# The sum over the partitions of a modulation chunk, placed one chunk later

## The chip, the cores and the metric

The kernel runs on one core of one Trainium2 chip. The metric is device time in microseconds (us), from the start of the program to its end. The kernel before takes 983.03 us (median of 3 runs, 981.76 to 984.24). The engines are TensorE (PE, with PEld for its weight loads), VectorE (DVE), ScalarE (ACT), GpSimd (POOL) and SyncE (SP), which issues most of the DMAs.

## What is computed

One layer of an encoder trunk with 512 tokens of width 1024, all in f32. A conditioning vector `c` gives six modulation vectors; each is 1024 long, and the last four of them are what this change is about:

```python
mod = silu(c) @ ada_w + ada_b                     # (1, 6 * 1024)
sh1, sc1, gt1, sh2, sc2, gt2 = split(mod, 6)
h = rmsnorm(x, g1) * (1 + sc1) + sh1
x = x + gt1 * mixer(h)                            # gated delta rule + mLSTM, both directions
h = rmsnorm(x, g2) * (1 + sc2) + sh2
x = x + gt2 * moe(h)                              # 32 experts, two for each token
out = rmsnorm(x, g3)
```

The mixer projects `h` with a wide matrix, runs the two recurrent branches over chunks of the sequence, and joins them. `gt1` is needed at the mixer's end, `sh2`, `sc2` and `gt2` after it.

## The kernel before

The kernel first makes `sh1` and `sc1`, normalises `x`, and begins the projection. One projection tile is 128 output columns for all 512 tokens: 24 matmuls (L347 to L349), eight contraction blocks with three products each of high and low halves of the operands. The halves of a weight tile, `w_hi` and `w_lo`, are split off by DVE, ACT or POOL (L145, L143, L150).

What the change touches lies in the middle of the run, about 190 to 580 us. There five strands of work are woven by a string written out by hand, `ORDER_B` (used at L1188): `g` is a projection tile for a gate, `p` prepares the delta rule's inverse, `s` is a step of its scan (L1033 to L1094), `m` is a step of the mLSTM (L821 to L955), and `d` is one chunk of the later modulation vectors. The strand `d` occurs 16 times: once as the first letter, then after twelve `g` and more, and then at ever shorter distances. `ORDER_C` follows with the rest of `m`, the first output branch `f` and operands `b`, and after it `mod_rows` (L803).

A chunk `q` (of 16, 256 columns of one modulation vector) goes like this. SP loads two halves of the weight's chunk, `aw`, of 512 KB each (L781, two buffers). Eight blocks of 128 rows are multiplied by a column of `silu(c)` and added up, with the rows on the partitions. In eleven chunks DVE does this in one accumulator `ac` (L788 for the first block, L790 for the other seven; one buffer). In chunks 2, 6, 14 and 15 ACT multiplies in place (L786) and DVE adds (L792, L795, L796); in chunk 4 ACT multiplies and POOL adds. In these five the sum stays in `aw` itself. Then TensorE sums over the partitions with a column of ones (L800; the profile shows four matmuls and four weight loads for a chunk, since f32 goes in two passes), and DVE copies the two columns of the result from PSUM into `mcols` (L801). `mod_rows` turns `mcols` (L806), adds the bias and writes the vectors to DRAM, from where `modb` and others are loaded (L1222).

The order on each engine in this part isn't the program's. It is worked out when the program is built, by a planner that has an estimated cost for each instruction: an instruction that stands earlier in the program goes first when both could start, and one that isn't ready by the planner's reckoning is passed over for a later one that is. On the chip each engine then takes its instructions strictly in that order, and waits where an operand isn't there yet. A buffer of a tile pool is given to the next tile once the last reader of the old one is done, so the first write into `ac` (L788) of a chunk comes after the sum (L800) of the chunk that had the buffer before.

Of the kernel before, what the change touches and what calls it, by code (L numbers as in the profile page):

```python
# [7 lines left out]
F32 = mybir.dt.float32  # L8
# [3 lines left out]
OP = mybir.AluOpType  # L12
# [91 lines left out]
def hybrid_kernel(tc, ins, out, consts_in):  # L104
    nc = tc.nc
    ctx = ExitStack()
    with ctx:
        _body(tc, nc, ctx, ins, out, consts_in)


def _body(tc, nc, ctx, ins, out, consts_in):
# [4 lines left out]
    def eng(key, default, choices):  # L116

        return CHOICE.get(key, default)
# [8 lines left out]
    def ps(tag, shape=None):  # L127
        uid[0] += 1
        n, b = psum["tags"][tag]
        return psum["pool"].tile([128, n], F32, name=f"ps_{tag}{uid[0]}", tag=tag, bufs=b)  # L130
# [6 lines left out]
    def nb(key, default, *choices):  # L137
        return eng("#" + key, default, (default,) + choices)
# [233 lines left out]
    for d in range(2):  # L372
# [16 lines left out]
                    op=OP.mult)  # L389
# [371 lines left out]
    pmd = stM.enter_context(tc.tile_pool(name="modw", bufs=1, side="right"))  # L761
# [9 lines left out]
    def mod_chunk(q):  # L771
        i, c0 = q // 4, (q % 4) * 256
        blk = MODS[i]
        o = blk * D + c0
        way = eng(f"mod{q}", "v", "vab")
        wt = []
        if way == "v":
            acc = pmd.tile([128, 256], F32, name=f"ac{q}", tag="ac", bufs=nb("ac", 1, 2))
        for h in range(2):
            w = pmd.tile([128, 4, 256], F32, name=f"aw{q}_{h}", tag="aw", bufs=nb("aw", 2, 3))  # L780
            DMA.dma_start(w, ada_w[h * 512:h * 512 + 512, o:o + 256].rearrange("(k p) n -> p k n", p=128))  # L781
            wt.append(w)
            for k in range(4):
                kk = h * 4 + k
                if way != "v":
                    A.activation(w[:, k], w[:, k], AF.Copy, scale=cT[:, kk:kk + 1])  # L786
                elif kk == 0:
                    V.tensor_scalar(acc, w[:, k], cT[:, kk:kk + 1], None, op0=OP.mult)  # L788
                else:
                    V.scalar_tensor_tensor(acc, w[:, k], cT[:, kk:kk + 1], acc, op0=OP.mult, op1=OP.add)  # L790
            if way != "v":
                (V if way == "a" else G).tensor_tensor(w[:, 0:2], w[:, 0:2], w[:, 2:4], op=OP.add)  # L792
        if way != "v":
            E = V if way == "a" else G
            E.tensor_tensor(wt[0][:, 0:2], wt[0][:, 0:2], wt[1][:, 0:2], op=OP.add)  # L795
            E.tensor_tensor(wt[0][:, 0], wt[0][:, 0], wt[0][:, 1], op=OP.add)  # L796
            acc = wt[0][:, 0]
        p = ps("m")
        for j in range(2):
            PE.matmul(p[:, j:j + 1], acc[:, j * 128:j * 128 + 128], ones[:, 0:1], start=True, stop=True)  # L800
        V.tensor_copy(mcols[:, q * 2:q * 2 + 2], p[:, 0:2])  # L801
# [7 lines left out]
        DMA.dma_start(mdr.rearrange("i (k p) -> (i k) p", p=128), mrow2[:, 0])  # L809

    def mod_chunks():
        for q in range(16):
            mod_chunk(q)
            yield

    stB = ctx.enter_context(ExitStack())
    pb = stB.enter_context(tc.tile_pool(name="mlstm", bufs=1, side="right"))
# [357 lines left out]
    def second_branch():  # L1175
# [7 lines left out]
        for j2 in range(4):  # L1183
            branch_out(ins["w_branch_b"][0], 4, j2, merge)
            yield

    todo.update({"p": prep(), "s": scan(), "m": mlstm(), "d": mod_chunks()})
    for c in ORDER_B:  # L1188
        take(todo[c], 1)
# [844 lines left out]
    last = NT - 1  # L2034
# [58 lines left out]
```

## Time and profile before

| what | value |
|---|---|
| median of 3 runs | 983.03 us (981.76 to 984.24) |
| profiled execution | 980.42 us, its span 978.6 us |
| PE busy | 814.2 us (83%) |
| DVE busy | 660.8 us (68%) |
| ACT, POOL busy | 328.1 us, 316.6 us |
| granted TensorE clock, mean | 0.924 of full speed |
| all L790 (DVE, 77 times) | 44.0 us, mean 572 ns |

The span runs from the first to the last instruction of the profiled execution. A busy time is the union of an engine's instructions, and a share is of the span. The shares hide that the stages differ: in the middle part DVE is busier than PE, and from 530 us on PE is.

### The profile page before, as it was taken

To read this page: it belongs to the slowest core of one execution; us is meant where nothing else is said; L and a number is where in the kernel's file an instruction comes from. 1 tells how busy PE (TensorE), PEld (TensorE's weight loads), DVE (VectorE), ACT (ScalarE), POOL (GpSimd) and SP (SyncE) were. 2 spreads that over 40 slices of the span, in tenths; PEclk is the share of its full clock that TensorE was granted. 3 is DMA by queue.
4 is the path that set the end of the run, shared out by engine and by line. 5 is a ranking of instruction groups with operands and counts; after the bars stand their busy time and mean duration, and the time that the engine had idled before them with its cause. 6 is when DMAs were issued, how large, how long until landed. Compare 5 with 4: busy or idle time off the path is not lost.

```text
span 978.6 us, 16538 instructions
## 1 busy us (share of the span) xinstructions
PE 814.2 (83%) x6204; PEld 595.0 (61%) x6204; DVE 660.8 (68%) x1246; ACT 328.1 (34%) x611; POOL 316.6 (32%) x236
## 2 busy tenths in 40 slices
PE   4799979979486999988797998987699999999840
PEld 3367656768375777866675776776456555555420
DVE  1459999799959999888888888459965322221215
ACT  5435475223101342321334231125522323333203
POOL 0321365214224442563236252323112212111125
PEclk9799999989786999998898999998899999999985
DMA  9932564975265365654474254946689999999965
GB/s 307 270 88 71 108 119 97 204 206 180 58 143 158 87 216 146 181 171 142 150 220 149 94 157 132 369 166 215 237 288 358 351 371 403 414 417 413 415 259 211
DMA packets 171709, 213.80 MB, mean 218 GB/s; under 512 B 47368, under 2 KB 129828, under 8 KB 171628
## 3 DMA queue, kind: packets, MB, share of 16 engines
q1 hardware_dynamic: 167340, 204.33, 64.6%
q0 software_dynamic: 4288, 8.41, 2.4%
q8 instruction: 49, 0.80, 0.3%
q14 instruction: 32, 0.26, 0.1%
HBM read 190.79 MB, written 25.54 MB: 221 GB/s over the span
## 4 chain that ended last, share of the span: by engine, by line
PE 41%; DVE 31%; DMA 16%; issue 5%; POOL 3%; ACT 2%; SPq 1%; POOLq 0%; DVEq 0%; ACTq 0%
DMA wr<-in_w_gate_dram 5%; PE ps_m L1705 5%; DMA wr<-in_w_up_dram 4%; PE ps_acc L348 3%; PE ps_acc L347 3%; PE ps_acc L349 3%; DMA wr<-in_w_down_dram 3%; DVE gu L740 2%; PE ps_m L1708 2%; PE ps_d L1736 2%; DVE ac L790 2%; DVE tt L742 2%; DVE ca L573 1%; PE ps_m L902 1%; DMA hb<-h1d 1%
## 5 line engine op out<-in xcount | busy, mean ns | idle before, releaser
L349 PE MATMUL ps_acc<-hn_hi,w_lo 128*128 128x512 f32 x352 | 142.6, 405 | 16.2 <-DVE w_lo L150 15.4
L347 PE MATMUL ps_acc<-hn_hi,w_hi 128*128 128x512 f32 x352 | 145.5, 413 | 1.8 <-DVE w_hi L145 1.3
L348 PE MATMUL ps_acc<-hn_lo,w_hi 128*128 128x512 f32 x352 | 145.0, 412 | 0.0
L1705 PE MATMUL ps_m<-wr,xin 128*64 128x256 f32 x1024 | 124.4, 390 | 6.1 <-ACT xin L1695 4.2
L150 POOL TENSOR_TENSOR w_lo<-w_raw,w_hi 128x1024 fp32r<-128x1024 f32 x34 | 88.1, 2590 | 103.2 <-ACT w_hi L143 80.9
L1714 DVE SCALAR_TENSOR_TENSOR act<-act,ps_m 64x256 f32<-64x256 f32 (+1 forms) x32 | 14.8, 463 | 133.0 <-ACT act L1713 133.0
L1705 PEld LDWEIGHTS ps_m<-wr,xin 128*64 128x64 f32 x1024 | 75.0, 139 | 43.3 <-issue 6.8
L349 PEld LDWEIGHTS ps_acc<-hn_hi,w_lo 128*128 128x128 f32 x352 | 68.7, 195 | 32.1 <-DVE w_lo L150 16.6
L347 PEld LDWEIGHTS ps_acc<-hn_hi,w_hi 128*128 128x128 f32 x352 | 68.8, 196 | 17.5 <-issue 3.2
L348 PEld LDWEIGHTS ps_acc<-hn_lo,w_hi 128*128 128x128 f32 x352 | 68.8, 195 | 15.6 <-issue 1.5
L1752 POOL DMA_INDIRECT ybuf<-y,idxp x28 | 27.3, 974 | 132.7 <-DVE y L1747 123.8
L1736 PE MATMUL ps_d<-wr,at 128*64 128x512 f32 x256 | 61.3, 598 | 5.2 <-DMA wr<-in_w_down_dram 4.0
L1695 ACT ACTIVATE xin<-xall (+1 forms) x128 | 54.2, 424 | 13.8 <-issue 9.5
L1713 ACT ACTIVATE act<-ps_m 64x256 f32<-64x256 f32 (+1 forms) x32 | 13.4, 418 | 134.7 <-PE ps_m L1705 71.1
L143 ACT ACTIVATE w_hi<-w_raw 128x1024 fp32r<-128x1024 f32 x30 | 31.7, 1058 | 57.3 <-PE ps_acc L348 43.5
L790 DVE SCALAR_TENSOR_TENSOR ac<-aw,cT,ac 128x256 f32<-128x256 f32 x77 | 44.0, 572 | 0.6
L1752 POOL DMA_INDIRECT ybuf<-y,idx x16 | 15.9, 992 | 74.6 <-DVE y L1747 61.1
L1747 DVE TENSOR_TENSOR y<-ps_d,gt 128x512 f32<-128x512 f32 (+1 forms) x32 | 25.3, 792 | 21.4 <-PE ps_d L1736 16.7
L1736 PEld LDWEIGHTS ps_d<-wr,at 128*64 128x64 f32 x256 | 17.4, 136 | 30.0 <-issue 20.1
L1725 PEld LDWEIGHTS ps_m<-ident,act 64*128 64x128 f32 x128 | 16.5, 186 | 22.4 <-DVE act L1715 12.6
L1497 PE MATMUL ps_acc<-woh,yT 128*128 128x512 f32 x64 | 27.5, 430 | 0.0
L740 DVE TENSOR_TENSOR gu<-nn,tt 128x62 f32<-128x62 f32 (+15 forms) x31 | 27.0, 870 | 0.7
(550 smaller groups left out, 1788.0 us busy)
## 6 DMA issues: line engine op xcount, KB each, us to landing
wr<-in_w_gate_dram SPq DMA_DIRECT2D x64, 512.0 KB
wr<-in_w_up_dram SPq DMA_DIRECT2D x64, 512.0 KB
wr<-in_w_down_dram SPq DMA_DIRECT2D x32, 1024.0 KB
w_raw<-in_w_in_dram SPq DMA_DIRECT2D x48, 512.0 KB
aw<-in_ada_w_dram SPq DMA_DIRECT2D x32, 512.0 KB
adaw<-in_ada_w_dram SPq DMA_DIRECT2D x8, 1024.0 KB
gts<-gt SPq DMA_DIRECT2D x20, 256.0 KB
gts<-gts SPq DMA_DIRECT2D x20, 256.0 KB
```

The source lines that it names most:

```text
L143: A.activation(dst, src, AF.Copy, **({} if scale is None else {"scale": scale}))
L150: ENGINE[eng(key, default, choices)].tensor_tensor(dst, a, b, op=op)
L347: PE.matmul(p, hi[:, k], hn_hi[:, k], start=(k == 0), stop=False)
L348: PE.matmul(p, hi[:, k], hn_lo[:, k], start=False, stop=False)
L349: PE.matmul(p, lo[:, k], hn_hi[:, k], start=False, stop=(k == KD - 1))
L740: V.tensor_tensor(o, nn_[:, :, m:, c].unsqueeze(3).to_broadcast([128, 2, n, m]), tt[:, :, c, 0:m].unsqueeze(2).to_broadcast([128, 2, n, m] ...
L790: V.scalar_tensor_tensor(acc, w[:, k], cT[:, kk:kk + 1], acc, op0=OP.mult, op1=OP.add)
L1497: PE.matmul(p, yT[0][:, k, ts], hi[:, k % 2], start=(k == 0), stop=False)
L1695: A.activation(xg[:, :, o], xall[:, :, bass.ds(vs[t], SEG)], AF.Copy)
L1705: PE.matmul(p[64 * b:64 * b + 64, 0:256], xg[:, kk, 0:64], r[:, b], **f)
L1736: PE.matmul(p[64 * c:64 * c + 64, 0:512], at[:, j, 0:64], w[:, j * D + c * 512:j * D + c * 512 + 512], start=(j == 0), stop=(j == 1))
L1752: return G.indirect_dma_start(out=ybuf.rearrange("r (a n) -> (r a) n", a=parts), out_offset=bass.IndirectOffsetOnAxis(ap=ix, axis=0), in_= ...
```

## The change

`mod_chunk(q)` ends with its accumulation and returns the accumulator; the two matmuls and the copy from PSUM become a function of their own, `mod_sum`. The strand `d` calls `mod_sum` for chunk `q-1` right before it issues chunk `q`, and for chunk 15 when the strand is asked once more, after everything in `ORDER_C`. The accumulator `ac` keeps one buffer, and chunks 2, 4, 6, 14 and 15 now write their last addition into it too.

```diff
         wt = []
-        if way == "v":
-            acc = pmd.tile([128, 256], F32, name=f"ac{q}", tag="ac", bufs=nb("ac", 1, 2))
+        acc = pmd.tile([128, 256], F32, name=f"ac{q}", tag="ac", bufs=1)
...
             E.tensor_tensor(wt[0][:, 0:2], wt[0][:, 0:2], wt[1][:, 0:2], op=OP.add)
-            E.tensor_tensor(wt[0][:, 0], wt[0][:, 0], wt[0][:, 1], op=OP.add)
-            acc = wt[0][:, 0]
+            E.tensor_tensor(acc, wt[0][:, 0], wt[0][:, 1], op=OP.add)
+        return acc
+
+    def mod_sum(q, acc):
+
         p = ps("m")
         for j in range(2):
             PE.matmul(p[:, j:j + 1], acc[:, j * 128:j * 128 + 128], ones[:, 0:1], start=True, stop=True)
...
     def mod_chunks():
+        last = None
         for q in range(16):
-            mod_chunk(q)
-            yield
+            if q:
+                mod_sum(q - 1, last)
+            last = mod_chunk(q)
+            yield
+        mod_sum(15, last)
```

## Rows read from the trace of the kernel before

**Rows 1.** The busy time of each engine by stage. The columns are the stretch, its length, then for each engine its busy time and count, then the granted clock, the DMA share and GB/s.

```profile
202.00:268.00 66.00, 52.09 (x220) 42.08 (x220) 64.26 (x75) 16.86 (x26) 20.58 (x9) 0.89 0.49 142
...
330.00:370.00 40.00, 35.78 (x440) 29.60 (x440) 34.84 (x64) 15.17 (x29) 19.22 (x19) 1.00 0.62 185
370.00:400.00 30.00, 29.50 (x188) 24.38 (x186) 29.08 (x54) 10.38 (x17) 8.51 (x5) 1.00 0.55 156
...
420.00:450.00 30.00, 21.95 (x125) 17.47 (x125) 27.39 (x42) 5.92 (x9) 15.42 (x10) 0.89 0.46 138
450.00:482.00 32.00, 27.16 (x239) 21.93 (x238) 26.91 (x53) 7.18 (x13) 8.87 (x6) 0.84 0.52 157
...
500.00:530.00 30.00, 23.41 (x143) 19.84 (x144) 26.32 (x43) 12.99 (x28) 14.06 (x12) 0.89 0.56 173
530.00:560.00 30.00, 27.95 (x190) 22.88 (x190) 25.76 (x57) 10.53 (x16) 13.07 (x9) 1.00 0.37 117
560.00:580.00 20.00, 19.94 (x90) 15.80 (x89) 15.95 (x26) 6.45 (x8) 9.40 (x6) 1.00 0.60 165
```

**Rows 2.** The chain that ended last, between 444 and 452 us: start, length, what.

```profile
444.62 1.17 DVE ac L790
...
448.54 0.41 DVE ac L790
449.08 0.99 PE ps_m L800 x4
450.07 0.64 PE ps_acc L347
```

**Rows 3.** The waits of PE between 180 and 530 us: who waited for whom, us in total, times, the longest.

```profile
PE ps_m L800 <- DVE ac L790: 13.4, 4, 4.8
...
PE ps_m L800 <- issue: 5.1, 2, 3.9
```

**Rows 4.** The same of DVE between 196 and 580 us.

```profile
DVE mcols L801 <- PE ps_m L800: 4.5, 6, 1.3
...
DVE z L1077 <- PE ps_c L1069: 2.4, 2, 1.4
```

**Rows 5.** TensorE in order of time around the sum of chunk 9: start, length, operation, and in brackets the idle time before it and what ended it.

```profile
428.20 0.39 PE L348 MATMUL ps_acc<-hn_lo,w_hi 128*128 128x512 f32 x1
432.28 0.58 PE L800 MATMUL ps_m<-ones,ac 128*128 128x1 f32 x4 [3.70 <-DVE ac L790]
432.72 0.49 PE L349 MATMUL ps_acc<-hn_hi,w_lo 128*128 128x512 f32 x1
...
434.20 0.63 PE L347 MATMUL ps_acc<-hn_hi,w_hi 128*128 128x512 f32 x1
```

**Rows 6.** DVE in order of time around the same sum.

```profile
431.66 0.47 DVE L790 SCALAR_TENSOR_TENSOR ac<-aw,cT,ac 128x256 f32<-128x256 f32 x1
...
432.90 0.16 DVE L801 COPY mcols<-ps_m 128x2 f32<-128x2 f32 x1 [0.16 <-PE ps_m L800]
432.98 0.35 DVE L788 TENSOR_SCALAR ac<-aw,cT 128x256 f32<-128x256 f32 x1
```

**Rows 7.** The sum of chunk 0 on TensorE, and its copy on DVE.

```profile
201.32 0.99 PE L800 MATMUL ps_m<-ones,ac 128*128 128x1 f32 x4 [3.91 <-issue]
...
202.34 0.16 DVE L801 COPY mcols<-ps_m 128x2 f32<-128x2 f32 x1 [0.77 <-PE ps_m L800]
```

**Rows 8.** Chunk 1: the last block of its accumulation on DVE, and its sum on TensorE.

```profile
217.35 0.48 DVE L790 SCALAR_TENSOR_TENSOR ac<-aw,cT,ac 128x256 f32<-128x256 f32 x1
...
290.49 0.61 PE L800 MATMUL ps_m<-ones,ac 128*128 128x1 f32 x4
```

**Rows 9.** Chunk 4's last addition on POOL and its sum on TensorE; the first and the last block of chunk 5 on DVE and its sum.

```profile
337.73 1.70 POOL L796 TENSOR_TENSOR aw<-aw 128x256 f32<-128x256 f32 x1
...
369.16 0.50 PE L800 MATMUL ps_m<-ones,aw 128*128 128x1 f32 x4
...
343.59 0.35 DVE L788 TENSOR_SCALAR ac<-aw,cT 128x256 f32<-128x256 f32 x1
...
361.25 1.50 DVE L790 SCALAR_TENSOR_TENSOR ac<-aw,cT,ac 128x256 f32<-128x256 f32 x1
...
373.67 0.50 PE L800 MATMUL ps_m<-ones,ac 128*128 128x1 f32 x4
```

**Rows 10.** Line L790 alone by stage: the stretch, its length, DVE's busy time in it and the count, clock, DMA.

```profile
290.00:330.00 40.00, 6.19 (x7) 0.79 0.46 126
330.00:370.00 40.00, 4.29 (x7) 1.00 0.62 185
370.00:400.00 30.00, 3.35 (x7) 1.00 0.55 156
```

**Rows 11.** The end of the strand: chunk 15's additions on DVE, its sum on TensorE, and the turning of `mcols`.

```profile
502.85 1.29 DVE L792 TENSOR_TENSOR aw<-aw 128x512 f32<-128x512 f32 x2
...
507.29 1.22 DVE L795 TENSOR_TENSOR aw<-aw,aw 128x512 f32<-128x512 f32 x1
...
508.96 0.42 DVE L796 TENSOR_TENSOR aw<-aw 128x256 f32<-128x256 f32 x1
...
525.62 0.85 PE L800 MATMUL ps_m<-ones,aw 128*128 128x1 f32 x4
...
577.10 0.27 PE L806 MATMUL ps_m<-ident,mcols 128*32 128x128 f32 x1
```

## The prediction

> **What bounds the kernel now.** Read first the busy time by stage. From 202 to 268 us DVE works 64.26 us of 66 and PE 52.09; from 420 to 482 us DVE works 54.30 of 62 (27.39 and 26.91) and PE 49.11; from 530 us PE takes over, with 27.95 of 30 and then 19.94 of 20, while DVE has 25.76 and 15.95 [rows 1]. So in the part where the sixteen chunks run DVE is the bound, and after it PE. Second, the chain of waits at 444 to 452 us: a DVE multiply-add of a chunk (L790), then its sum on PE (L800), then a projection matmul [rows 2]. The chain goes over from DVE to PE at a chunk's sum. Third, the waits. PE stood 13.4 us in four waits for L790 and 5.1 us in two more, put down to "issue", all ahead of L800 [rows 3]. DVE stood far less because of it: 4.5 us at the copy L801 and 2.4 us at the scan's L1077 [rows 4]. As DVE is the bound there, these 6.9 us are what the sums cost at most, and not the 18.5 us of PE.
>
> Two things about the order matter. Chunk 9's sum stands in the middle of a projection tile, between L348 and L349, and PE waits 3.70 us for it [rows 5]: the planner put it where it took the accumulation to be done, and DVE was later. Chunk 1's sum on the other hand ran at 290.49 us although its accumulation had ended at 217.83, and chunk 4's at 369.16 though ready at 339.43 [rows 8, 9]: there PE had work of earlier rank, and the sum waited for its turn in the program. So a sum is late by its rank when DVE is ahead, and early by the planner's reckoning when DVE is behind. The change lowers the rank. It acts on the first kind directly, and on the second only if it makes the accumulation start no later.
>
> **The change, part by part.** The same 64 matmuls, 16 copies and 5 last additions run; nothing is added but the place of five results, and the cost of that is nil (the same operands and shape). I work against the profiled execution, 980.42 us with a span of 978.6 and so 1.82 us outside it. The median shown, 983.03, lies 2.61 above it; differences are added to the median.
>
> *Chunk 0.* Its sum loses its rank to twelve gate tiles, but at 201.32 us PE had been idle for 3.91 us, as the first gate tile's weights weren't split yet. An idle engine is given what is ready, so I expect the sum in the same place. The copy L801, now of a later rank, goes behind the splitting of the weights; DVE's wait of 0.77 us [rows 7] goes: 0.8 us off a stage in which DVE has 1.74 us to spare. If I am wrong and the sum goes behind the gate tiles, chunk 1's accumulation can't start before about 290 us, and eight operations at about 0.48 us, 3.8 us, leave that stage for a later one in which DVE is the bound too: nothing won in sum. From 0 to -3.8 us; I take -0.8.
>
> *The accumulator.* It has one buffer, and L788 of a chunk writes it first. Before, it followed at once on the sum and copy of the chunk ahead (432.28, 432.90, 432.98) [rows 5, 6]. Now sum `q-1` has the rank of chunk `q`, and so has L788 of chunk `q` behind it. Sum, accumulation, sum: this ring is what it was, one place later. For chunks 8 to 13, where DVE is behind, PE has passed their ranks already, and lowering them by one chunk doesn't move the sum: it is still put where the planner takes it for ready. I expect the waits of 3.70 us and the like to remain, at other chunks. From all 4.5 + 2.4 us won to nothing; I take nothing.
>
> *Chunks 4 and 5.* Chunk 4's sum stays in `aw` now, so chunk 5 could begin on `ac` at 343.59 us and end at 362.75. After the change chunk 4's result takes `ac`, its sum has chunk 5's rank, 369 to 374 us, and chunk 5 can't begin until then [rows 9]. Its 0.35 + 4.29 us [rows 9, 10] leave a stage in which DVE is busy 34.84 of 40 for one of 29.08 of 30 or 27.39 of 30 [rows 1]. What one stage wins the next pays: nothing, unless the same operations take longer there. They took 6.19 us for seven at 290 to 330 us and 3.35 at 370 to 400 [rows 10], so that one chunk can cost 2.8 us more or, from 4.29, 0.9 us less: -0.9 to +2.8, and I take nothing, as the stage it goes to has the cheap row.
>
> [...]
>
> *Behind them.* Chunk 5's start moves from 343.59 to 369.66 us at the earliest, the end of chunk 4's sum [rows 9], 26 us. If the chunks behind it keep that delay, sum 15, at 525.62, comes at 552 us. `mod_rows` turns the result at 577.10 [rows 11], so 25 us of cover remain. If they were gone, PE would wait for L806 in its order, microsecond for microsecond. Chunk 15's additions, 1.29 + 1.22 + 0.42 = 2.93 us [rows 11], would leave the stretch 500 to 530 for one bound by PE. DVE idles 3.68 us of that stretch anyway, so I take half, -1.5 us, with ends at 0 and -2.9.
>
> *The queues.* SP gets the loads of `aw` in an order that the planner makes anew; the loads of chunks 3, 7 and 15 no longer wait for a sum, but for the last addition, which waits for the sum before. One wait stands for the other: 0. Behind L788 on DVE are conv, scan and mLSTM work, which wait with it as they did with L801.
>
> The sum: -0.8 + 0 + 0 - 1.5 + 0 = -2.3, and 983.03 - 2.3 = 980.7 us.
>
> **The rivals.**
>
> *The waits go.* If the lowered ranks do put the sums behind their accumulations, DVE gets back its 4.5 and 2.4 us, and with the 1.5 of the strand's end the time is 983.0 - 8.4 = 974.6. For it: after the wait for chunk 9, whose stretch had a granted clock of 0.89, projection matmuls took 0.63 us where they took 0.39 before it [rows 1, 5], so a shorter wait frees more of PE than itself. Against it: the one buffer, by which DVE starts a chunk no earlier.
>
> *DVE waits instead* (the slower side). Place: L788 of the eleven chunks and L796 of the other four on DVE, 15 instructions which now wait for a sum that PE reaches later by rank, with all of DVE's queue behind them. Price: the wait at L801 was 0.75 us on average (4.5 over 6) and 1.3 at the longest [rows 4]; 15 times 0.75 is 11.3, less the 4.5 paid now 6.8, and 989.8 us; 15 times 1.3 gives 19.5, less 4.5 is 15, and 998. It decides from the point at which DVE's idle time ended by L800 passes 7.5 us. For it: sums of chunks 1 and 4 that waited 73 and 30 us for their turn. Against it: the planner passes over an L788 whose sum it hasn't placed.
>
> *Nothing moves.* If the sums are placed by readiness throughout, the ranks change little, and the time is 983.0.
>
> **How the numbers follow.** A time within 0.3% (2.95 us) of 983.03 can't be told from no change here. The forecast, 980.7, has 0.42; the waits go, 0.22; DVE waits, 0.26; nothing moves, 0.10. A planner that re-orders a thousand instructions scatters the forecast by its own bounds: -0.8 to 0 at chunk 0, -0.9 to +2.8 for the contended chunk, -2.9 to 0 at the end, 978.4 to 985.8. Of its 0.42 I give 0.15 to faster by more than 0.3%, 0.24 to within it and 0.03 to slower. Faster: 0.15 + 0.22 = 0.37. Within: 0.24 + 0.10 = 0.34. Slower: 0.03 + 0.26 = 0.29. The range goes from below the first rival's 974.6 to the second's middle price, since its upper half is the least likely: 972 to 992.
>
> **What would show it.** In the profile of the changed kernel the sum of chunk 0 still stands at about 201 us and the copy behind it costs DVE no wait; chunk 5's L788 comes after 369 us; PE still waits over 8 us in all for L790 ahead of L800; the last sum comes at 540 to 560 us, ahead of L806. The prediction is wrong if PE's waits ahead of L800 fall under 4 us and DVE's idle time with them, if DVE's waits ended by L800 grow past 7.5 us, or if L806 has to wait.

## The result, and the profile after

The changed kernel takes 989.31 us (median of 20 runs, 986.32 to 992.83); the kernel before, on the same chip, 983.01 us. The ratio is 1.0079, with a 95% interval of 1.0063 to 1.0096: 6.3 us slower, where 2.3 us faster had been forecast. The profiled execution of the changed kernel took 991.87 us, with a span of 990.1; it lies 2.56 us above its median, and the one of before 2.59 under its own. So 5.2 of the 11.5 us between the two profiles are not in the medians. They arise behind 600 us: by the same PE instructions the two profiles stand about 6 us apart there and 11 at 660 us. One execution of each can't tell whether that rest is scatter; what follows is about the part ahead of it.

The busy time by stage, with the columns of [rows 1]:

```profile
202.00:268.00 66.00, 52.72 (x220) 42.64 (x220) 64.51 (x75) 16.84 (x26) 21.58 (x10) 0.89 0.52 150
...
330.00:370.00 40.00, 36.95 (x447) 30.21 (x446) 33.69 (x62) 13.86 (x27) 22.66 (x21) 1.00 0.54 159
370.00:400.00 30.00, 29.43 (x192) 24.20 (x190) 25.52 (x47) 12.37 (x21) 7.29 (x4) 1.00 0.61 177
...
420.00:450.00 30.00, 24.68 (x154) 19.53 (x154) 24.81 (x44) 5.62 (x8) 14.25 (x10) 0.89 0.50 144
450.00:482.00 32.00, 24.84 (x232) 19.78 (x231) 27.46 (x52) 7.43 (x15) 8.86 (x7) 0.84 0.50 148
...
500.00:530.00 30.00, 23.46 (x118) 20.05 (x119) 23.84 (x42) 12.37 (x25) 12.71 (x10) 0.77 0.59 177
530.00:560.00 30.00, 25.95 (x162) 21.39 (x161) 26.25 (x55) 9.39 (x17) 13.86 (x9) 0.89 0.47 149
560.00:580.00 20.00, 19.64 (x98) 15.74 (x97) 15.91 (x29) 4.46 (x7) 5.53 (x5) 1.00 0.40 119
```

Against [rows 1], DVE worked less in three stages: 25.52 of 30 us instead of 29.08 at 370 to 400 (where PE, with 29.43 and 29.50, is as full), 24.81 instead of 27.39 at 420 to 450, 23.84 instead of 26.32 at 500 to 530. At 450 to 482 it worked more, 27.46 instead of 26.91. Then PE, which had worked 27.95 of 30 us at 530 to 560, has 25.95, and its granted clock there is 0.89 instead of 1.00.

DVE's waits between 196 and 580 us, against [rows 4] (who waited for whom, us in total, times, the longest):

```profile
DVE hb L150 <- POOL mu L177: 8.3, 4, 4.4
DVE mcols L803 <- PE ps_m L802: 7.8, 8, 3.3
```

The first of them in the kernel before:

```profile
DVE hb L150 <- POOL mu L177: 5.2, 4, 1.6
```

And PE's, ahead of the sums (now L802) between 180 and 530 us, against [rows 3]:

```profile
PE ps_m L802 <- DVE ac L789: 7.7, 2, 3.9
PE ps_m L802 <- DVE ac L795: 7.1, 1, 7.1
...
PE ps_m L802 <- issue: 2.4, 1, 2.4
```

PE waits 17.2 us ahead of the sums, before 18.5. DVE waits 7.8 us at the copies, before 4.5, and 8.3 us for GpSimd's `mu`, before 5.2, a wait for which the prediction has no term. The change moved PE's waits to other chunks and lengthened DVE's.

**Where the 6 us come in.** At the transposes of the third pair (L945, now L951) the kernels are even, 524.74 and 525.18 us. At the last turn of the first branch's exchange (L613) they stand at 551.99 and 558.97, and at the transposes of the fourth pair the difference is still 6.9 us (571.04 and 577.98). So 6.5 us come in within this one passage of the profiled executions. TensorE in it, in order of time (start, length, operation, and in brackets the idle time and what ended it), first of the kernel before:

```profile
536.21 1.47 PE L608 MATMUL ps_c<-ident,gg 128*128 128x128 f32 x12
...
539.45 0.52 PE L608 MATMUL ps_c<-ident,gg 128*128 128x128 f32 x3 [1.56 <-DVE gts L1154]
...
540.40 0.27 PE L843 MATMUL ps_m<-ident,qk 128*128 128x128 f32 x1
...
542.30 0.73 PE L1125 MATMUL ps_acc<-brT,br_hi 128*128 128x512 f32 x2
```

and of the changed kernel:

```profile
538.62 1.47 PE L608 MATMUL ps_c<-ident,gg 128*128 128x128 f32 x12
...
544.25 0.87 PE L608 MATMUL ps_c<-ident,gg 128*128 128x128 f32 x3 [4.05 <-DVE gts L1160]
...
545.67 0.42 PE L849 MATMUL ps_m<-ident,qk 128*128 128x128 f32 x1
...
549.31 0.71 PE L1131 MATMUL ps_acc<-brT,br_hi 128*128 128x512 f32 x2
```

Three things are to be seen. The exchange begins 2.4 us later, as PE still had 48 projection matmuls to do ahead of it, before 38. PE then waits 4.05 us for DVE, before 1.56. And after that wait PE is slow: a turn of `qk` takes 0.42 us instead of 0.27, and from the end of the wait to the first branch matmuls it is 5.06 us instead of 2.85 (549.31 - 544.25 and 542.30 - 539.45), with a granted clock of 0.50 in these 5.06 us and 1.00 in the 2.85. 2.4, 2.5 and 2.2 make 7.1 us; 0.4 us of it the kernels stood apart at the start already, which leaves 6.7 for the 6.5 measured. The kernels were even at the third pair's transposes by that instruction alone: PE came there with ten projection matmuls less done.

Why DVE was late there, its own rows say. First before, then after:

```profile
521.78 2.82 DVE L150 TENSOR_TENSOR hb<-hb,mu 128x512 f32<-128x512 f32 x1 [0.91 <-POOL mu L177]
...
531.57 0.23 DVE L1147 TENSOR_SCALAR rn<-rn 128x8 f32<-128x8 f32 x2
...
538.46 1.62 DVE L1154 TENSOR_TENSOR gts<-gts,ps_c 64x256 f32<-64x256 f32 x4
```

```profile
524.34 0.69 DVE L150 TENSOR_TENSOR hb<-hb,mu 128x512 f32<-128x512 f32 x1 [1.18 <-POOL mu L177]
...
526.95 0.42 DVE L795 TENSOR_TENSOR ac<-aw 128x256 f32<-128x256 f32 x1
...
527.94 0.69 DVE L150 TENSOR_TENSOR gg<-gg,rn 128x512 f32<-128x512 f32 x1
528.54 2.39 DVE L1153 TENSOR_SCALAR rn<-rn 128x8 f32<-128x8 f32 x1
...
533.30 1.01 DVE L888 TENSOR_TENSOR rm<-rm,cst 128x512 f32<-128x512 f32 x1
...
541.10 2.25 DVE L147 TENSOR_SCALAR hn_hi<-bt,gcol 128x512 fp32r<-128x512 f32 x1 [0.23 <-DMA bt<-btd]
543.26 1.62 DVE L1160 TENSOR_TENSOR gts<-gts,ps_c 64x256 f32<-64x256 f32 x4
```

From the end of `hb` to the exchange's additions DVE needs 13.9 us before (524.60 to 538.46) and 18.2 after (525.03 to 543.26). It has work there that the kernel before had done by then: chunk 15's last addition, `gg` and `rm`, with one more conv tap, come to 2.9 us. And two instructions take longer: one `rn` takes 2.39 us where two took 0.23 before, and a second `hn_hi` takes 2.25 where the one ahead of it took 1.26 (and one of the kernel before, at 555.72 us with GpSimd idle, 0.48). Eight `rm` (L892) take 3.05 us where seven (L886) took 2.00. Against these stand one `hn_lo` less, 1.42 us, and 2.0 us less of idle time, 0.23 instead of 2.21.

### The profile page after: what moved, and what is told of

It is laid out like the page before. It is cut to its first block, busy times and chain, and to the rows that moved or that the text cites. A ratio compares the mean times of both kernels' runs of the same rounds, so it can differ in the third digit from the quotient of the medians.

```text
span 990.1 us, 16541 instructions
## 1 busy us (share of the span) xinstructions
PE 827.5 (84%) x6204; PEld 607.0 (61%) x6204; DVE 659.7 (67%) x1246; ACT 327.0 (33%) x611; POOL 319.4 (32%) x236
## 5 line engine op out<-in xcount | busy, mean ns | idle before, releaser
L1720 DVE SCALAR_TENSOR_TENSOR act<-act,ps_m 64x256 f32<-64x256 f32 (+1 forms) x32 | 14.8, 463 | 133.3 <-ACT act L1719 121.5
L789 DVE SCALAR_TENSOR_TENSOR ac<-aw,cT,ac 128x256 f32<-128x256 f32 x77 | 45.6, 592 | 0.4
L1731 PEld LDWEIGHTS ps_m<-ident,act 64*128 64x128 f32 x128 | 16.5, 186 | 22.7 <-DVE act L1721 13.4
L1504 PE MATMUL ps_acc<-wol,yT 128*128 128x512 f32 x64 | 27.3, 426 | 0.2 <-POOL wol L150 0.2
```

The costliest lines, as they stand in the source:

```text
L1504: PE.matmul(p, yT[0][:, k, ts], lo[:, k % 2], start=False, stop=False)
```

## The experiments

Ratios are to the kernel before in the same batch. The theories as they came up: **R**, the ring through the one accumulator makes DVE or PE wait; **D**, the delay of the sums does it; **N**, any new order of this part costs, whatever the edit; **F**, chunk 4's result in `ac` keeps chunk 5 back; **S**, the late chunks stand ahead of the scan's last step; **C**, the loss belongs to this change and not to re-planning; **L** and **M**, it belongs to the last three chunks, or to the whole strand. In the first four texts below theory 1 is D with S, theory 2 is R and theory 3 is N, and their times are for a kernel before of 983 us. Every edit also makes a new order on the engines, so a gain can hide behind what the new order costs; the swaps below show what that can be.

**The two halves of the change.** First the delay alone, with the five results left in `aw`:

```diff
-        acc = pmd.tile([128, 256], F32, name=f"ac{q}", tag="ac", bufs=1)
+        if way == "v":
+            acc = pmd.tile([128, 256], F32, name=f"ac{q}", tag="ac", bufs=1)
...
-            E.tensor_tensor(acc, wt[0][:, 0], wt[0][:, 1], op=OP.add)
+            E.tensor_tensor(wt[0][:, 0], wt[0][:, 0], wt[0][:, 1], op=OP.add)
+            acc = wt[0][:, 0]
```

> The sums come one chunk later, but the five results stay in the weight's buffer as before. Theory 1: 988 to 990 us, the scan's last step at 508 us or later. Theory 2: 983 to 985. Theory 3: anywhere from 976 to 990.

Measured: 984.14 us, 1.0040 (1.0013 to 1.0066). For a kernel before of 983 us that is 986.9, between theories 1 and 2.

Then the results in `ac` alone, with every sum at its old place; in effect:

```diff
         for q in range(16):
-            if q:
-                mod_sum(q - 1, last)
-            last = mod_chunk(q)
+            acc = mod_chunk(q)
+            mod_sum(q, acc)
             yield
-        mod_sum(15, last)
```

> The sums stay where they were before; only the results of chunks 2, 4, 6, 14 and 15 go into the one accumulator. Theory 1 (the strand of chunks is one chunk late, and the DVE work of chunks 13 to 15 lies ahead of the scan's last step): no delay, so 983 us within 2 us, and the scan's last step on TensorE at about 502 us. Theory 2 (the five results in the one buffer add waits): about 989 us, with a wait of several us ahead of the sum of chunk 2. Theory 3 (every new plan scatters by as much as this change did): anywhere from 976 to 990.

Measured: 996.37 us, 1.0169 (1.0129 to 1.0209), or 999.6 us for 983, which is over what any theory gave. The 7.1 us of waiting ahead of chunk 2's sum are there, but the change has them too. D can't be the whole cause, as this kernel has no delay. The half that the prediction priced at nothing, the place of five results, costs twice as much alone as the whole change does, and the delay, which costs 0.4% alone, takes half of it back. The effects don't add up (0.40 + 1.69 against 0.79).

The delay for the first seven sums alone, and for the last nine alone, with all results in `ac`. The edit, and with `q >= 7` the other one:

```diff
         for q in range(16):
-            if q:
+            if last is not None:
                 mod_sum(q - 1, last)
-            last = mod_chunk(q)
+                last = None
+            acc = mod_chunk(q)
+            if q < 7:
+                last = acc
+            else:
+                mod_sum(q, acc)
             yield
-        mod_sum(15, last)
+        if last is not None:
+            mod_sum(15, last)
```

> Sums of chunks 0 to 6 one chunk later, those of 7 to 15 at their old place, all results in the accumulator. Theory 1: the strand has caught up by 500 us, so 983 to 985 us. If the loss comes from the early part (the 7 us wait ahead of chunk 2's sum): 988 to 990. Theory 3: anywhere from 976 to 990.

> Sums of chunks 0 to 6 at their old place, those of 7 to 15 one chunk later. Theory 1: 988 to 990 us, the scan's last step at 508 us or later. If the loss comes from the early part: 983 to 985. Theory 3: anywhere from 976 to 990.

Measured: 985.54 us, 1.0050 (1.0022 to 1.0079), and 989.9 us, 1.0092 (1.0064 to 1.0121), or 987.9 and 992.0 us for 983. The first is at the edge of what was put for an early loss, the second over what was put for a late one; its scan's last matmul came at 516.4 us, as theory 1 has it. Neither end of the strand is free.

**Two accumulators.** A second buffer of `ac` takes the ring away. It needs room, so `rows`, `cols` and `th8` move to another pool. The change with the room alone, then with the buffer, then the kernel before with it, then the results in `ac` with it:

```diff
-    rows = sm.tile([64, 128], F32, name="rows")
+    rows = p0.tile([64, 128], F32, name="rows")
...
-        acc = pmd.tile([128, 256], F32, name=f"ac{q}", tag="ac", bufs=1)
+        acc = pmd.tile([128, 256], F32, name=f"ac{q}", tag="ac", bufs=2)
```

> The change as made, with the three small tiles of the start moved as for the second accumulator, but one accumulator still. All theories but N: as the change, 0.8% slower than before. Theory N: up to 1.7% either way.

> The change as made, with two accumulators. Theory R: within 0.3% of before, or up to 0.5% faster, as the sums then find their accumulation done. Theory D: 0.4% slower, as with the delay alone. Theory N: up to 1.7% either way.

> The kernel before with two accumulators (the same tiles moved). Theory R: as before or up to 0.5% faster, as chunks 8 to 13 no longer wait for one another's sums. Theory D: as before. Theory N: up to 1.7% either way.

> Sums at their old place, all sixteen results in the accumulator as in the run that took 1.7% longer than before, but with two accumulators (the room for the second comes from three small tiles of the start, moved to a pool that closes early). Theory R (the single buffer: a chunk can't start before TensorE has summed the chunk ahead, and DVE loses what it fills its gaps with): within 0.3% of before. Theory D (the delay by one chunk): also within 0.3%, as there is no delay, but then the 1.7% of the run with one buffer has no cause. Theory N (each new plan scatters): up to 1.7% either way.

Measured, in this order: 1.0060 (1.0031 to 1.0089), 1.0095 (1.0064 to 1.0127), 1.0054 (1.0027 to 1.0081) and 1.0194 (1.0144 to 1.0244). The room alone leaves the order of PE, DVE, ACT and POOL as it is, and it repeats the change's ratio within the intervals. The buffer takes waits away: PE's for the accumulations go from 14.8 to 3.8 us in the change and from 13.4 to 7.1 in the kernel before, DVE's at the copies from 7.8 to 5.5 and from 4.5 to 4.4. The changed kernel's DVE at 392 us waits for chunk 5's sum, which stands in PE's order behind a run of projection matmuls, with chunk 6's last write into `ac` queued behind:

```profile
392.43 0.69 DVE L794 TENSOR_TENSOR aw<-aw,aw 128x512 f32<-128x512 f32 x1
396.47 0.16 DVE L803 COPY mcols<-ps_m 128x2 f32<-128x2 f32 x1 [3.34 <-PE ps_m L802]
396.55 0.41 DVE L795 TENSOR_TENSOR ac<-aw 128x256 f32<-128x256 f32 x1
```

With two buffers the same write comes without a wait:

```profile
396.97 0.34 DVE L892 SCALAR_TENSOR_TENSOR rm<-rm,aa,cst 128x128 f32<-128x128 f32 x1
397.24 0.41 DVE L795 TENSOR_TENSOR ac<-aw 128x256 f32<-128x256 f32 x1
```

and DVE, the third busy time of the window's row, works 28.22 us of the 30 from 370 to 400 instead of 25.52:

```profile
370.00:400.00 30.00, 27.45 (x178) 22.64 (x178) 28.22 (x51) 12.62 (x25) 7.96 (x6) 1.00 0.55 158
```

Yet the time doesn't fall in any of the three pairs. So R isn't the whole cause: most of PE's waits in the ring can go without a gain. That they cost nothing isn't shown, as the buffer makes a new order too, and the room alone was run with the change only.

**Chunk 4.** Its result back in `aw`, first with the sums at their old place, then in the change:

```diff
+        if way != "b":
             acc = pmd.tile([128, 256], F32, name=f"ac{q}", tag="ac", bufs=1)
...
+            if way == "b":
+                acc = wt[0][:, 0]
             E.tensor_tensor(acc, wt[0][:, 0], wt[0][:, 1], op=OP.add)
```

> The sums at their old place, the results of chunks 2, 6, 14 and 15 in `ac`, chunk 4's left in `aw`, so that chunk 5 may begin on `ac` before chunk 4's sum, as before the change. With all five results in `ac` the time was 1.7% over the kernel before. Theory F (the result of chunk 4 in `ac` keeps DVE's work of chunk 5 out of the stretch 343 to 363 us and puts it into 370 to 450): chunk 5's sum comes back from 381 to about 374 us, and the time falls to within 0.7% of the kernel before. Theory N (any plan made anew is some tenths of a per cent to two per cent worse, whatever the edit): it stays anywhere between 0.4% and 1.9% over. The prediction's step (chunks 4 and 5 cost nothing): no change against 1.7%.

> The change, with chunk 4's result left in `aw`. Theory F: chunk 5's additions return to about 343 to 363 us, ahead of chunk 4's sum, the DVE filler that was lost before 400 us comes back, and the time is under 0.3% over the kernel before, or even with it. If the delay alone sets the time (0.4% with all five results left in `aw`), this gives 0.4%. Theory N: 0.4% to 1.9% over.

Measured: 1.0152 (1.0105 to 1.0200) and 1.0074 (1.0026 to 1.0122). In the first, chunk 5 did begin at 346.10 us instead of 370.26, and the ratio fell by 0.17%, within the intervals. In the second chunk 5 began at 370.25 instead of 374.65, still behind chunk 3's sum (367.93), so that one tells little. F is out as the main cause.

**The scan's last step.** One letter moved in the changed kernel, and the same in the kernel before:

```diff
-ORDER_B = "dggggggggggggmggmppppdmddmpmmgmsdgsmdmmgdsmdmmsddmdsmdmsmddgsmdmgmmdmsmgm"
+ORDER_B = "dggggggggggggmggmppppdmddmpmmgmsdgsmdmmgdsmdmmsddmdsmdmsmddgssmdmgmmdmmgm"
```

> The change, with the last letter `s` of the order string (step 7 of the scan) ahead of the letter `d` of chunk 14 and two letters `m`. Theory S (the 7 us arise because DVE's work of chunks 13 to 15 stands ahead of the scan's last step, whose last matmul went from 502.4 to 509.7 us): the last matmul of the scan comes at 503 us or earlier, the exchange of the first branch ends some 5 to 7 us earlier than 559 us, and the time is within 0.3% of the kernel before. Theory N: the time stays 0.4% or more over the kernel before, whenever the scan ends.

> The kernel before with the same letter moved and nothing else: a control for the planning. Theory S: the scan's last step is not late there (502.4 us), so moving it up gains nothing that reaches the end: within 0.3%. Theory N: the plan made anew costs 0.4% or more, without any sum or accumulator having been touched.

Measured: 1.0075 (1.0046 to 1.0104) and 1.0057 (1.0029 to 1.0086). The scan's last matmul came at 485.7 and 485.2 us instead of 509.7 and 502.4, and nothing was won: the exchange's last turn in the change came at 561.35 us, where S wanted it 5 to 7 us ahead of 559. In the kernel before the move cost 0.57%. S is out as put; a gain of up to what the move costs by itself could hide behind it. N gained a point here, as no chunk had been touched in the second; the next four runs took it away again.

**Four swaps of neighbouring letters** in the kernel before, none of them a `d`: at the start, in the middle at two places, and at the end of the string.

```diff
-ORDER_B = "dggggggggggggmggmppppdmddmpmmgmsdgsmdmmgdsmdmmsddmdsmdmsmddgsmdmgmmdmsmgm"
+ORDER_B = "dgggggggggggmgggmppppdmddmpmmgmsdgsmdmmgdsmdmmsddmdsmdmsmddgsmdmgmmdmsmgm"
+ORDER_B = "dggggggggggggmggmppppdmddmpmmgmsdgmsdmmgdsmdmmsddmdsmdmsmddgsmdmgmmdmsmgm"
+ORDER_B = "dggggggggggggmggmppppdmddmpmmgmsdgsmdmmgdsmdmsmddmdsmdmsmddgsmdmgmmdmsmgm"
+ORDER_B = "dggggggggggggmggmppppdmddmpmmgmsdgsmdmmgdsmdmmsddmdsmdmsmddgsmdmgmmdmsmmg"
```

> The kernel before, with the second `m` of the order string one gate tile later (`mggm` to `mgggm` with one `g` fewer ahead of it). Theory N: 1.003 to 1.006. Theory C: 0.998 to 1.002.

> The kernel before, with one `s` of the scan and the `m` behind which it stood swapped, between chunks 7 and 8 of the order string. Theory N: 1.003 to 1.006. Theory C: 0.998 to 1.002.

> The kernel before, with one `s` and the `m` ahead of it swapped, just before chunks 9 and 10 of the order string. Theory N: 1.003 to 1.006. Theory C: 0.998 to 1.002.

> The kernel before, with the last two of its order string's letters, `g` and `m`, swapped: the last gate tile comes after the last step of the mLSTM. Theory N (the order before is one well-placed draw, and nearly any other costs): 1.003 to 1.006 of the kernel before. Theory C (the loss of the change comes from its sums and results): 0.998 to 1.002.

Measured, in this order: 0.9995 (0.9966 to 1.0025), 1.0017 (0.9987 to 1.0048), 0.9983 (0.9948 to 1.0019) and 1.0090 (1.0065 to 1.0116). Three new orders cost nothing that is clear of the noise, as C has it, so N is out as put; the fourth, which differs only at the end, costs as much as the change, so C is wrong for the end of the strand.

**The change split at chunk 13.** All but the last three chunks, then the last three alone, each with `if q < 13` or `if q >= 13` in the loop above and the results in `ac` for the same chunks:

```diff
-        acc = pmd.tile([128, 256], F32, name=f"ac{q}", tag="ac", bufs=1)
+        own = way == "v" or q < 13
+        if own:
+            acc = pmd.tile([128, 256], F32, name=f"ac{q}", tag="ac", bufs=1)
```

> The change for chunks 0 to 12; chunks 13, 14 and 15 are summed at their old place, and the results of 14 and 15 stay in `aw`. Theory L (the loss is made by the last three chunks, whose additions, sums and two results stand around the scan's last step and the exchange of the first branch): the exchange ends at 552 to 554 us instead of 559, and the time is 0.998 to 1.003 of the kernel before. Theory M (the loss is made of many small displacements over the whole strand): 1.004 to 1.010.

> The kernel before, with chunks 13, 14 and 15 alone summed one place later, and the results of 14 and 15 in `ac`. Theory L: the exchange ends at 557 us or later, and the time is 1.005 to 1.009 of the kernel before. Theory M: under 1.003.

Measured: 1.0087 (1.0055 to 1.0118) and 1.0048 (1.0023 to 1.0072). The last three alone nearly reach L's range, though their exchange's last turn came at 554.42 us and not at 557 or later. Without them it came at 548.87, ahead of L's 552 to 554, and yet the loss is as large as the change's. It comes in behind: PE waits for DVE again, and takes 0.63 us for a matmul that takes 0.39 from 567 us on, the granted clock of 550 to 570 us being 0.59.

```profile
556.62 0.80 PE L1143 MATMUL ps_acc<-brT,br_lo 128*128 128x512 f32 x1 [5.27 <-DVE br_lo L150]
557.21 0.63 PE L1141 MATMUL ps_acc<-brT,br_hi 128*128 128x512 f32 x1
```

So L is out as the only cause, and M is right for the first run and wrong for the second.

**What all of them share.** The stage from 530 to 580 us, in which PE is the bound, tells the kernels that lose from those that don't. The busy time of that window (columns as in [rows 1]) before, after, with the second middle pair swapped (0.9983), with the late pair swapped (1.0090), and without the change's last three chunks (1.0087):

```profile
530.00:580.00 50.00, 47.89 (x278) 38.67 (x278) 41.70 (x82) 16.99 (x23) 22.47 (x15) 1.00 0.46 136
```

```profile
530.00:580.00 50.00, 45.59 (x258) 37.12 (x257) 42.16 (x83) 13.85 (x23) 19.39 (x14) 0.93 0.44 137
```

```profile
530.00:580.00 50.00, 47.91 (x278) 38.52 (x276) 43.05 (x79) 15.29 (x21) 23.50 (x15) 1.00 0.41 117
```

```profile
530.00:580.00 50.00, 44.47 (x241) 35.67 (x240) 37.13 (x69) 12.97 (x19) 15.79 (x12) 0.90 0.37 116
```

```profile
530.00:580.00 50.00, 41.21 (x211) 33.45 (x210) 35.44 (x72) 13.06 (x24) 15.79 (x11) 0.76 0.29 89
```

The same figures for all kernels, from one profiled execution each:

| kernel | ratio | DVE busy, 202 to 530 us | PE busy, 530 to 580 us | its clock there |
|---|---|---|---|---|
| before | 1 | 287.6 | 47.9 | 1.00 |
| early pair swapped | 0.9995 | 288.0 | 47.9 | 1.00 |
| middle pair swapped | 1.0017 | 286.5 | 47.9 | 0.99 |
| second middle pair swapped | 0.9983 | 288.5 | 47.9 | 1.00 |
| delay alone | 1.0040 | 283.5 | 47.6 | 0.97 |
| last three chunks alone | 1.0048 | 287.8 | 45.2 | 0.93 |
| delay of sums 0 to 6 | 1.0050 | 284.2 | 46.0 | 0.88 |
| before, two buffers | 1.0054 | 278.7 | 47.1 | 0.93 |
| before, scan's last step first | 1.0057 | 288.4 | 44.8 | 0.97 |
| change, room made | 1.0060 | 279.7 | 45.6 | 0.93 |
| change, chunk 4 in `aw` | 1.0074 | 284.1 | 45.6 | 0.93 |
| change, scan's last step first | 1.0075 | 280.3 | 43.0 | 0.93 |
| **the change** | 1.0079 | 278.7 | 45.6 | 0.93 |
| change but the last three | 1.0087 | 282.9 | 41.2 | 0.76 |
| late pair swapped | 1.0090 | 286.4 | 44.5 | 0.90 |
| delay of sums 7 to 15 | 1.0092 | 286.8 | 47.4 | 0.95 |
| change, two buffers | 1.0095 | 279.4 | 43.8 | 0.93 |
| results in `ac`, but chunk 4's | 1.0152 | 281.5 | 39.5 | 0.90 |
| results in `ac` | 1.0169 | 282.9 | 41.9 | 0.90 |
| results in `ac`, two buffers | 1.0194 | 280.0 | 43.8 | 0.93 |

The four that keep their time have PE at 47.9 of 50 us and a clock of 0.99 or 1.00; all sixteen that lose have less than either. The table sorts the kernels, by one execution each and after their times were known. It doesn't give the size of a loss and doesn't show a cause: a fixed window cuts a stage that itself moves, and a kernel that is late has other work in it.

Nor does the loss come in at one place. From the exchange's first turn to 570 us the longest wait of PE for DVE is 1.54 to 1.56 us in the four that keep their time, and 4.0 to 6.7 us in eight of the sixteen: at the same turn in the change, with the room made, with two buffers, with chunk 4 in `aw`, with the scan's last step first and with the last three alone, at 542.48 us in the late swap (4.67), and at 556.62 in the change without the last three (5.27). In the other eight it is 2.3 us at most. The three with the results in `ac` and the sums at their old place were late ahead of it: their third pair's transposes stand at 536.43 to 541.51 us instead of 524.74. The delay of sums 0 to 6 has the exchange's last turn at 551.18, ahead of 551.99, and loses behind it. By the fourth pair's transposes the losses are there, in about the order of the ratios: these stand at 568.35 to 573.69 us in the four and at 573.25 to 589.48 in the sixteen.

DVE's busy time from 202 to 530 us, under 285 us in the change and eleven others, is no measure of work left over. The change without the last three has 451 instructions there with 282.9 us, as many as the kernel before (450), and the delay of sums 7 to 15 has 442 with 286.8, as many as the change (443).

No version ran faster than the kernel before; the second middle swap, at 0.9983, can't be told from it.

**What stays open.** Which single displaced instruction starts DVE's lag in the change wasn't isolated. That the wait and the slow clock make the loss is read from the traces; no run takes the wait alone away, or the long `rn` and `hn_hi`. Nor was why the results in `ac` cost most with the sums at their old place, with one accumulator and with two. The swaps that cost nothing also moved less: compared in order of time by their tiles, with repeats taken together, 1 to 19 of the 1,035 steps of the kernel before on DVE have lost their place in the order, 99 in the change. What an order as much displaced would cost without any chunk touched, no run shows; the late swap, with 15, shows that place counts too.

## Why the prediction was wrong

*Chunk 0*: right. Its sum stands at 201.34 us, and the copy comes behind the splitting of the weights, without a wait:

```profile
202.50 1.22 DVE L150 TENSOR_TENSOR w_lo<-w_raw,w_hi 128x1024 fp32r<-128x1024 f32 x1
...
204.15 0.16 DVE L803 COPY mcols<-ps_m 128x2 f32<-128x2 f32 x1
```

The 0.8 us that go there show as 64.51 us of DVE work in the stage instead of 64.26, 0.25 us.

*The accumulator*: about right for PE. For L790 (now L789) its waits are 7.7 us, just under the 8 named, and 14.8 with the additions of L795, which now write `ac`. Wrong for DVE: DVE's waits at the copies were taken as they were; they went from 4.5 to 7.8 us, past the 7.5 that had been named as the point from which "DVE waits instead" decides. That rival's time, 989.8, is nearly the measured 989.31, but its mechanism is not what the runs bear out. It had the waits at the first write into `ac`; no such write on DVE waited for a sum, the copy ahead did (396.47). Its price was 6.8 us more of DVE's waits, and there were 3.3 more. The agreement in time is by chance.

*Chunks 4 and 5*: about right. Chunk 5 began at 374.65 us, after the 369 named, and its seven blocks went to the stage with the cheap row, where they took 3.30 us instead of 4.29. Its first block took 1.93 instead of 0.35, so the chunk cost 0.6 us more, within the bounds of -0.9 to +2.8. The forecast's range calls it the contended chunk; no run shows what it would contend with. In the kernel with the results in `ac` alone, chunk 5 back at 346 us left the time the same within the intervals.

```profile
374.65 1.93 DVE L787 TENSOR_SCALAR ac<-aw,cT 128x256 f32<-128x256 f32 x1
```

*Behind them*: this step failed. It had the chunks 26 us late and the last sum at 552 us. Sums 9 to 13 came 6 to 12 us later than before, and the last one at 584.03, past the 540 to 560 named, since its rank was behind everything in `ORDER_C`. That by itself cost nothing, as `mod_rows` follows it without a wait:

```profile
584.03 0.50 PE L802 MATMUL ps_m<-ones,ac 128*128 128x1 f32 x4
...
585.63 0.27 PE L808 MATMUL ps_m<-ident,mcols 128*32 128x128 f32 x1
```

What failed is the sentence that chunk 15's additions would "leave the stretch 500 to 530 for one bound by PE", and the -1.5 us taken for it. They didn't leave: they stand at 509.67, 511.19, 513.19 and 526.95 us.

```profile
509.67 0.69 DVE L791 TENSOR_TENSOR aw<-aw 128x512 f32<-128x512 f32 x1
...
513.19 0.68 DVE L794 TENSOR_TENSOR aw<-aw,aw 128x512 f32<-128x512 f32 x1
```

DVE worked less in that stretch all the same, and what it left was other work. A stage with PE busy 27.95 of 30 us [rows 1] was read as one in which DVE's work is covered. But that PE was so busy there rested on DVE having been on time: the exchange, the branch operands and the last pair's products all come from DVE. DVE came to 530 us with 8.9 us less of busy time (278.7 against 287.6). At the median time of each form in the twenty traces, an estimate, 4.6 us of it are work not done; the rest is instructions that took less long. Ten projection matmuls more, one wait of 4.05 us and the slow clock behind it are what came instead. In place of -1.5 this term measured +6.5 in the profiled executions, in the passage from 525 to 559 us. That is near the 6.3 us of the medians; that the other terms came to nothing isn't shown one by one.

*The place of five results*: "the cost of that is nil" failed too. In `ac` alone they cost 1.69%, and the change costs 0.79% where the delay alone costs 0.40%, which leaves about 3.8 us for them, with intervals that just overlap. The operations are the same, as the prediction says; their order isn't.

*The queues*: "One wait stands for the other: 0" holds for SP, where no wait for a load of `aw` shows up among DVE's largest. The sentence behind it, that conv, scan and mLSTM work wait behind L788 "as they did with L801", names where DVE's 3.3 us of additional waits went, and gave them no price.

The scatter of the planning was put as 978.4 to 985.8 us, -2.3 to +5.1 around the forecast, with little chance of slower than before. The controls show nothing to +0.9% (9 us), and no order of the eighteen that was reliably better.

## What to carry to other kernels

Where an engine is busy nine tenths of a stage, look at what feeds it before counting its busy time as cover: what the feeding engine brings late into that stage can be paid there, as here with 4.05 us of wait where there were 1.56, and with 2.2 us behind it at a granted clock of 0.50 instead of 1.00; what lowers the clock, no run shows. Before a wait is priced, ask whether removing it alone would move the end; here a second accumulator took away 11.0 of PE's 14.8 us of waits for the accumulations and won nothing. And where a planner orders the work, measure a few edits that shouldn't matter, at the start, in the middle and at the end: here four runs showed three places where a swap cost nothing and one where it cost 0.9%.

## What the hardware showed that was not expected

A DVE instruction on 128x8 elements took 2.39 us where the same line took 0.15 to 0.17 at its other places. It ended, at 530.93 us, with an instruction of GpSimd, at 530.90; `hn_hi`, 2.25 us, ended at 543.35, and GpSimd's next one at 543.05:

```profile
527.46 3.44 POOL L150 TENSOR_TENSOR w_lo<-w_raw,w_hi 128x1024 fp32r<-128x1024 f32 x1
...
540.65 2.40 POOL L150 TENSOR_TENSOR br_lo<-br_raw,br_hi 128x1024 fp32r<-128x1024 f32 x1
```

So `rn` took 2.2 us more than at its other places, and `hn_hi` 1.8 more than the 0.48 of the kernel before with GpSimd idle. The prediction has no term for it. That GpSimd held the two is read from these ends alone; no run takes the GpSimd instructions away. Beside another GpSimd instruction the same line took its usual time:

```profile
534.84 0.15 DVE L1153 TENSOR_SCALAR rn<-rn 128x8 f32<-128x8 f32 x1
```

```profile
533.72 2.08 POOL L177 TENSOR_TENSOR rn<-rn,half 128x8 f32<-128x8 f32 x1
```

In the profiles of the kernels before and after, five DVE instructions of this kind (a tensor with a scalar, on 128x8) began 0.3 us or more ahead of the end of a GpSimd instruction. This `rn`, within one of 1024 columns, took 2.39 us. Two within a GpSimd power on 128x8 took 0.16 (`mu`, at 519.80 us before) and 0.15 (`rn`, at 534.84 after), and two `gcol` within one of 512 columns took 0.15 each (165.59 before, 166.01 after). What tells the first from the other four, no run shows.

TensorE's clock gave the loss in the passage a second part. In the changed kernel PE had been idle for 4.05 us up to 544.25 and then took 0.42 us for a transpose that takes 0.27, the granted clock being 0.50 from 544.25 to 549.31 us and 0.83 from 530 to 550, before 1.00 in both. All sixteen kernels that lost show such a fall between 530 and 580 us, with mean clocks of 0.76 to 0.97, and of the four that didn't none is under 0.99.
